# The planner of a one-core hybrid layer: its clock, its step boundaries and the start of a front

## The chip, the cores and the metric

One core of a Trainium2 chip runs the whole program in one launch. The metric is device time in microseconds (us), the median of runs of the same program, and less is better. TensorE (PE) does the matmuls, VectorE (DVE), ScalarE (ACT) and GpSimd (POOL) the rest, and SyncE (SP) issues most of the DMAs.

## The reference, cut to what matters

One layer for a prompt of 16 + 1024 rows and a sample of 64 rows, all in fp32, the model 2048 wide:

```
xn   = rmsnorm(h) * norm_w
proj = xn @ w_in                                   # 2048 -> 8208
a_b, a_c, a_x, a_z, qkv, z_b, b_logit, a_logit = split(proj)
y_a  = a_b * causal_conv3(a_c * a_x) * silu(a_z)   # mixer A, 1024 channels
q, k, v = silu(causal_conv4(qkv))                  # mixer B, 8 heads x 128
q = l2norm(q) / sqrt(128);  k = l2norm(k)
S_t = exp(g_t) (I - beta_t k_t k_t^T) S_{t-1} + beta_t k_t v_t^T ;  o_t = S_t^T q_t
y_b = rmsnorm(o) * o_norm_w * silu(z_b)
h   = h + concat(y_a, y_b) @ w_out
y   = rmsnorm(h) * final_norm_w
```

The recurrence is computed in chunks: with A unit lower triangular (built from k k^T, beta and the decays), T = inverse(A), and per chunk u = T (beta v - beta exp(g) k S), o = exp(g) q S + (q k^T * decay) u, and a new S.

## The kernel before, in words

**Stages.** The 1104 rows (with a gap, 1152) are three pieces of three 128-row chunks, and they are kept transposed (features on partitions) in a high and a low fp32r half, as are the weights: a product is three matmuls (xh*wh, xl*wh, xh*wl). A *job* is one 128-column tile of `w_in` for all three pieces: 16 k-steps of nine matmuls into three PSUM tiles `pj` (four banks in all). Weight chunks of four k-steps come as `wr` by SP, ACT makes `wh` and DVE `wl` (`Weights.split`). When a job ends, `post` evicts its `pj` tiles on DVE and starts a generator (`a_tile`, `b_tile`, `z_tile`) for the convolution and the SiLU, whose result goes to DRAM (`scr`, `yscr`). At the end three passes of `block` multiply by `w_out`, `evac` adds the residual, and `finish` makes the final norm. For the last 512 columns the `w_out` tiles are loaded and split ahead by `after(1, ...)`: `wq`, then `wa`/`wb` (k below 12) or a free corner of `yh` (k from 12).

**The delta rule** runs between the projection's matmuls, 24 times (8 heads x 3 pieces), as a front and a back. `dn_front(h, p)` loads k and q (`kq`), transposes q (`psq`) and k (`psk`) on PE, takes sums of squares on ACT (`accum_out`, tile `ss`), and works out the scales on DVE (`rsqrt_of`, `cq`, `kn`); then masks `bm` and `at`, the products `psm`, and the 32x32 inverses: `bm` goes to DRAM (`e_in`), POOL eliminates in 30 steps, and the result comes back into `t32`. `dn_back(h, p)` reads `t32`, builds the 128x128 inverse (`psx`, `psy`), runs three chunks of the state (`psr`, `psu`, `psn`, `po`), then takes the norm of `po`: sums of squares on ACT (`jk`, `so2`, which the rows call `so`), fifteen small DVE operations (the first reads `so2`, the last makes `ro`, called `roy` in the rows) and `on`; then it transposes `on` on PE (`pot`) and multiplies by `zg`. The PSUM pool `psd` has three banks, and the one of `po` is its own.

**What sets the order.** Each engine works its instructions off in order. The DVE's order is the one in which the Python code issues them. The generators are interleaved by a planner: `clk` holds a planned time of PE, DVE and ACT. `mm` and `tr` add to `clk["pe"]`; `Timed` (V and S) adds a fixed part and a part per element to DVE's or ACT's. After each k-step of nine matmuls, `pump` advances every generator whose due time has come (`running[k][0] <= clk["pe"]`); a `yield d` sets the next due time to `max(clk.values()) + d`. Convolution steps are pumped while DVE's planned time is less than 0.7 us ahead of PE's, and what is left of them at the end of a job is issued there, ahead of the next evictions (`flush_convs`). A back may start when the planned end of POOL's work is reached (`EL`, `el_done`); a front f when `f - backs[0] <= 1`, `backs[0]` being the number of backs that have ended.

Of the kernel before, what the change touches and what calls it, by code (L numbers as in the profile page):

```python
# [8 lines left out]
F32 = mybir.dt.float32  # L9
# [8 lines left out]
P = 128  # L18
# [7 lines left out]
NG = 3 * NH  # L26
# [19 lines left out]
class Timed:  # L46
# [5 lines left out]
    def __getattr__(self, name):  # L52
        fn = getattr(self._e, name)

        def call(out, *a, **k):
            n = 1
            for d in out.shape[1:]:
                n *= d
            c = self._c
            c[self._k] = max(c[self._k], c["pe"]) + self._f + n * self._p  # L60
            return fn(out, *a, **k)  # L61

        return call
# [3 lines left out]
def hymba_kernel(ctx: ExitStack, tc: tile.TileContext, hT, x_prompt, x_sample, w_in, w_ba, w_out, cst1, cst2, par,  # L67
                 s_delta, fnw, y_p, y_s, o_ca, o_cq, o_dp, o_ds):
    nc = tc.nc
    clk = {"pe": 0.0, "dve": 0.0, "act": 0.0}  # L70
    V = Timed(nc.vector, clk, "dve", 0.09, 0.00104)
    S = Timed(nc.scalar, clk, "act", 0.2, 0.00083)
    G, T, Q = nc.gpsimd, nc.tensor, nc.sync

    def mm(out, lhsT, rhs, start, stop):
        n = 1
        for d in rhs.shape[1:]:
            n *= d
        if lhsT.dtype == F32R:
            clk["pe"] += max(n / 2400 + 0.003, 0.107)  # L80
        else:
            clk["pe"] += 4 * max(n, lhsT.shape[1]) / 2400
        T.matmul(out, lhsT, rhs, start=start, stop=stop)  # L83

    def tr(out, in_, idn):
# [53 lines left out]
    def rsqrt(y, t, v):  # L139

        V.tensor_scalar(t.bitcast(I32), v.bitcast(I32), 1, None, ALU.logical_shift_right)
        V.tensor_scalar(y.bitcast(I32), t.bitcast(I32), -1, 0x5F3759DF, ALU.mult, ALU.add)
        for _ in range(3):
            V.tensor_tensor(t, y, y, ALU.mult)
            V.scalar_tensor_tensor(t, t, -0.5, v, ALU.mult, ALU.mult)
            V.scalar_tensor_tensor(y, t, 1.5, y, ALU.add, ALU.mult)

# [20 lines left out]
    gens = []  # L168
    done = set()
    fronts, backs, el_done, front_of, state = [0], [0], {}, {}, {}  # L170
    running = {}
    pool_free = [0.0]

# [9 lines left out]
    def pump():  # L183
        while True:
            moved = False
            f, b = fronts[0], backs[0]
            if "gate" in done and "front" not in running and f < NG and f - b <= 1:
                h, p = divmod(f, 3)
                if (KQ, h, p) in done and (QQ, h, p) in done:
                    running["front"] = [0.0, dn_front(h, p)]  # L190
            if "back" not in running and b < f and b < NG and el_done.get(b, 1e9) <= clk["pe"]:
                h, p = divmod(b, 3)
                if (VQ, h, p) in done and (ZQ, h, p) in done:
                    running["back"] = [0.0, dn_back(h, p)]
            for k in list(running):
                if running[k][0] <= clk["pe"]:
                    moved = True
                    if not step(running[k]):
                        del running[k]
                        if k == "back":  # L200
                            backs[0] += 1
                        elif k == "front":
                            fronts[0] += 1
            if not moved:
                break
        while convs and clk["dve"] - clk["pe"] < 0.7:
            if not step(convs[0]):
                convs.popleft()
# [245 lines left out]
    with ExitStack() as pro:  # L454
# [80 lines left out]
        a, n = PIECES[0]  # L535
# [108 lines left out]
    with ExitStack() as pro:  # L644
# [10 lines left out]
        for p in range(3):  # L655
            a, n = PIECES[p]
# [99 lines left out]
    dn = net.enter_context(tc.tile_pool(name="dn", bufs=1))  # L756
# [6 lines left out]
    def psd(name):  # L763
        return pd.tile([P, 4, P], F32, tag="pd", name=name)

    EL = (5.0, 45.0)
    t32 = [dn.tile([P, 3, P], F32, tag=f"t32_{i}", name=f"t32_{i}") for i in range(2)]
    for i in range(2):
        V.memset(t32[i], 0.0)
# [2 lines left out]
    def dn_front(h, p):  # L772

        kq = tmp("kq", "kq", 2, (P, 3, 2, P))
        for i, w in ((0, KQ), (1, QQ)):
            Q.dma_start(kq[:, :, i, :], scr[h][w][p].rearrange("p (c t) -> p c t", t=P))
        gr = tmp("gr", "gr", 1)
        r0 = h * NCH + 3 * p
        Q.dma_start(gr, gscr[None, r0:r0 + 3, :].to_broadcast([P, 3, P]))
        yield 2.1  # L780
        c3 = slice(3 * p, 3 * p + 3)
        ss = dn.tile([P, 6], F32, tag="ss", name="ss", bufs=2)
        jk = dn.tile([P, P], BF16, tag="jk", name="jk")
        pq_ = psd("psq")
        for c in range(3):
            tr(pq_[:, c, :], kq[:, c, 1, :], ident)
        for c in range(3):
            S.activation(jk, pq_[:, c, :], AF.Square, accum_out=ss[:, 3 + c:4 + c])
        yield 0.0
        pk_ = psd("psk")  # L790
        for c in range(3):
            tr(pk_[:, c, :], kq[:, c, 0, :], ident)
        for c in range(3):
            S.activation(jk, pk_[:, c, :], AF.Square, accum_out=ss[:, c:c + 1])
        V.tensor_scalar(ss, ss, 4 * EPS, None, ALU.add)
        rq = rsqrt_of(dn, ss, 6, "rq")


        cq = dn.tile([P, 12], F32, tag="cq", name="cq", bufs=2)
        V.tensor_scalar(cq[:, 0:3], rq[:, 3:6], float(P) ** -0.5, None, ALU.mult)  # L800
        V.tensor_tensor(cq[:, 3:6], hb[:, h, c3], rq[:, 0:3], ALU.mult)
        V.tensor_tensor(rq[:, 3:6], rq[:, 0:3], rq[:, 0:3], ALU.mult)
        V.tensor_tensor(cq[:, 6:9], nbeg[:, h, c3], rq[:, 3:6], ALU.mult)
        V.tensor_tensor(cq[:, 9:12], nb[:, h, c3], rq[:, 3:6], ALU.mult)
        kn = tmp("kn", "kn", 2)
        V.tensor_tensor(kn, pk_[:, 0:3, :], kds[:, h, c3, None].to_broadcast([P, 3, P]), ALU.mult)
        km = None
        if p == 0:
            km = dn.tile([P, P], F32, tag="km", name="km")
            V.tensor_scalar(km, pk_[:, 0, :], kdm[:, h:h + 1], None, ALU.mult)  # L810
        yield 0.0

        bm = tmp("bm", "bm", 2)
        for c in range(3):
            cc = 3 * p + c
            V.scalar_tensor_tensor(bm[:, c, :], gr[:, c, :], gc[:, h, cc:cc + 1], cst[:, C_MS:C_MS + P], ALU.subtract,
                                   ALU.max)
        S.activation(bm, bm, AF.Exp, scale=-1.0)
        at = tmp("at", "at", 2)
        for c in range(3):  # L820
            cc = 3 * p + c
            V.scalar_tensor_tensor(at[:, c, :], gr[:, c, :], gc[:, h, cc:cc + 1], cst[:, C_MT:C_MT + P], ALU.subtract,
                                   ALU.min)
        S.activation(at, at, AF.Exp)
        S.activation(gr, gr, AF.Exp)
        if p == 0:

            V.memset(bm[64:P, 0, 0:64], 0.0)
            V.memset(at[0:64, 0, 64:P], 0.0)
        yield 0.0  # L830
        for c in range(3):
            pm = psd("psm")
            mm(pm[:, 0:2, :], kq[:, c, 0, :], kq[:, c, :, :], True, True)
            V.scalar_tensor_tensor(bm[:, c, :], pm[:, 0, :], cq[:, 9 + c:10 + c], bm[:, c, :], ALU.mult, ALU.mult)
            V.tensor_tensor(at[:, c, :], pm[:, 1, :], at[:, c, :], ALU.mult)
            yield 0.0
        yield 1.4

        eT = dn.tile([12, 32, 32], F32, tag="eT", name="eT", bufs=1)
        i = (3 * h + p) % 2  # L840
        Q.dma_start(whole(e_in[i]), bm)
        G.dma_start(eT, blocks(e_in[i]))  # L842
        tm = dn.tile([12, 240], F32, tag="tm", name="tm", bufs=1)
        for j in range(1, 31):
            n = 31 - j
            t = tm[:, 0:n * j].rearrange("m (i r) -> m i r", r=j)
            G.tensor_tensor(t, eT[:, j + 1:32, j:j + 1].to_broadcast([12, n, j]),  # L847
                            eT[:, j:j + 1, 0:j].to_broadcast([12, n, j]), ALU.mult)
            G.tensor_tensor(eT[:, j + 1:32, 0:j], eT[:, j + 1:32, 0:j], t, ALU.add)  # L849
        G.dma_start(blocks(e_out[i]), eT)  # L850
        G.dma_start(t32[i], whole(e_out[i]))
        yield 0.3

        V.tensor_tensor(kq[:, :, 1, :], kq[:, :, 1, :], gr, ALU.mult)
        front_of[h, p] = (kq, kn, km, at, cq, bm)
        pool_free[0] = el_done[3 * h + p] = max(clk["pe"] + EL[0], pool_free[0]) + EL[1]

    def dn_back(h, p):
        kq, kn, km, at, cq, bm = front_of.pop((h, p))
# [51 lines left out]
        for c in range(3):  # L911
# [31 lines left out]
            mm(po[:, c, :], kq[:, c, 1, :], s, False, True)  # L943
            state[h] = sn
            yield 0.2
        if p == 2:
            Q.dma_start(o_dp[h], state[h])

# [1 line left out]
        jk = dn.tile([P, P], BF16, tag="jk", name="jk")  # L950
        for c in range(3):
            S.activation(jk, po[:, c, :], AF.Square, accum_out=ss[:, c:c + 1])
        V.tensor_tensor(ss, ss, cq[:, 0:3], ALU.mult)
        V.scalar_tensor_tensor(ss, ss, 1.0 / P, cq[:, 0:3], ALU.mult, ALU.mult)
        V.tensor_scalar(ss, ss, EPS, None, ALU.add)
# [301 lines left out]
```

## Time and profile before

| | |
|---|---|
| median of 3 runs (lowest, highest) | 2252.47 us (2252.29, 2257.59) |
| the profiled execution | 2251.76 us; its span is 2250.0 us, so 1.76 us lie around it |
| PE busy | 2188.0 us, 97% |
| DVE, ACT, POOL busy | 1361.8 (61%), 602.4 (27%), 875.4 us (39%) |
| mean granted TensorE clock | 0.994 of full speed |

A PE matmul's record overlaps the next one (records of 340 ns follow each other every 174 ns), so PE's busy time says that little is idle, not how fast it goes. Times within the span are counted from its start. The clock of TensorE has two levels, 2.4 GHz (1.00) and 1.2 GHz (0.50).

### The profile page before, as it was taken

The page shows a single profiled execution, that of the slowest core. Times are in us where ns is not written, and L with a number is a line of the kernel's source. Part 1 is how long each engine was busy: PE and PEld are TensorE (multiplying, and loading weights), DVE is VectorE, ACT ScalarE, POOL GpSimd, SP SyncE. Part 2 cuts the span into 40 slices and gives each one's busy share as a digit, 9 for nine tenths or more (in the row PEclk, how much of TensorE's full clock was granted, in tenths as well). Part 3 has the DMA queues.
Part 4 walks back from the last instruction along what each step waited for, and adds up shares of the span by engine and source line. Part 5 has one row for each costly group of instructions (what it writes and reads, how often), then busy time and mean ns, then how long its engine had stood idle before and what let it go on. Part 6 is the DMA issues. An engine that isn't in the chain of part 4 may idle for free. (4 is left out here: it accounts for less than half of the span.)

```text
span 2250.0 us, 35424 instructions
## 1 busy us (share of the span) xinstructions
PE 2188.0 (97%) x12794; PEld 2071.4 (92%) x12794; DVE 1361.8 (61%) x3540; ACT 602.4 (27%) x1483; POOL 875.4 (39%) x1516
## 2 busy tenths in 40 slices
PE   8999999999999999999999999999999999999997
PEld 8999899999999999999999999999999997788886
DVE  6653475777585556665775567675645345474644
ACT  7232121222222212212222222222221125444341
POOL 0000038475556566666657655657473000000000
PEclk9999999999999999999999999999999999999999
DMA  7223132222222122223232223232221228664652
GB/s 262 78 87 94 39 92 81 84 86 89 84 88 81 56 81 88 81 59 90 72 99 64 81 75 87 85 87 78 72 74 53 94 82 279 207 198 145 225 166 85
DMA packets 162067, 231.12 MB, mean 103 GB/s; under 512 B 17756, under 2 KB 89636, under 8 KB 161764
## 3 DMA queue, kind: packets, MB, share of 16 engines
q1 hardware_dynamic: 156356, 217.30, 31.2%
q0 software_dynamic: 3072, 7.11, 1.7%
q10 hardware_dynamic: 2464, 4.46, 0.5%
q8 instruction: 100, 1.64, 0.3%
q14 instruction: 75, 0.61, 0.1%
HBM read 184.61 MB, written 44.17 MB: 102 GB/s over the span
## 5 line engine op out<-in xcount | busy, mean ns | idle before, releaser
L83 PE MATMUL pj<-xh,wh 128*128 128x384 f32 x2048 | 694.9, 340 | 11.5 <-DVE raw L61 3.9
L83 PE MATMUL pj<-xl,wh 128*128 128x384 f32 x2048 | 692.4, 338 | 1.3 <-DVE xl L61 1.3
L83 PE MATMUL pj<-xh,wl 128*128 128x384 f32 x2048 | 691.3, 338 | 0.0
L61 DVE TENSOR_TENSOR wl<-wr,wh 128x512 fp32r<-128x512 f32 x464 | 335.5, 725 | 343.6 <-ACT wh L61 341.0
L83 PE MATMUL pj<-x,wh 128*128 128x320 f32 (+3 forms) x2048 | 519.2, 333 | 6.6 <-ACT x L61 6.6
L61 ACT CAST wh<-wr 128x512 fp32r<-128x512 f32 x464 | 285.8, 618 | 845.5 <-PE pj L83 626.7
L847 POOL TENSOR_TENSOR tm<-eT 12x30 f32<-12x30 f32 (+4 forms) x720 | 399.6, 555 | 121.7 <-DMA eT<-e_in 67.1
L849 POOL TENSOR_TENSOR eT<-eT,tm 12x30 f32<-12x30 f32 (+4 forms) x720 | 422.9, 587 | 56.4
L83 PEld LDWEIGHTS pj<-xh,wh 128*128 128x128 f32 x2048 | 387.2, 189 | 17.3 <-DVE xt L61 4.8
L83 PEld LDWEIGHTS pj<-xl,wh 128*128 128x128 f32 x2048 | 387.0, 189 | 2.9 <-DVE xl L61 2.2
L83 PEld LDWEIGHTS pj<-xh,wl 128*128 128x128 f32 x2048 | 386.8, 189 | 0.0
L83 PEld LDWEIGHTS pj<-x,wh 128*128 128x128 f32 x2048 | 349.3, 190 | 12.6 <-ACT x L61 6.7
L83 PE MATMUL pj<-x,wl 128*128 128x320 f32 (+3 forms) x1024 | 320.4, 313 | 5.2 <-DVE wl L61 5.2
L842 POOL DMA_DIRECT2D eT<-e_in x24 | 17.2, 716 | 578.2 <-DMA wr<-in_w_in 310.8
L83 PE MATMUL po<-wh,yh 128*128 128x512 f32 x656 | 238.9, 396 | 1.6 <-DVE yh L61 1.5
L83 PE MATMUL po<-wl,yh 128*128 128x512 f32 x528 | 208.9, 396 | 1.8 <-DVE wl L61 1.7
L83 PEld LDWEIGHTS pj<-x,wl 128*128 128x128 f32 x1024 | 193.3, 189 | 7.1 <-DVE wl L61 6.6
L83 PEld LDWEIGHTS po<-wh,yh 128*128 128x128 f32 x656 | 123.1, 188 | 32.9 <-DVE yh L61 2.7
L61 DVE SCALAR_TENSOR_TENSOR acc<-raw,pk,acc 128x384 f32<-128x384 f32 (+1 forms) x216 | 147.1, 681 | 6.0
L83 PE MATMUL po<-wh,yl 128*128 128x512 f32 x336 | 132.8, 395 | 0.0
L83 PEld LDWEIGHTS po<-wl,yh 128*128 128x128 f32 x528 | 99.1, 188 | 27.5 <-DVE wl L61 4.0
L61 ACT ACTIVATE raw<-acc 128x384 f32<-128x384 f32 (+1 forms) x72 | 36.8, 512 | 154.2 <-DVE acc L61 154.2
(242 smaller groups left out, 2127.9 us busy)
## 6 DMA issues: line engine op xcount, KB each, us to landing
wr<-in_w_in SPq DMA_DIRECT2D x288, 256.0 KB, 3.1
wr<-in_w_out SPq DMA_DIRECT2D x176, 256.0 KB, 2.8
scr<-acc SPq DMA_DIRECT2D x48, 192.0 KB, 1.9
kq<-scr SPq DMA_DIRECT2D x48, 192.0 KB, 3.0
hres<-in_x_prompt SPq DMA_DIRECT2D x32, 256.0 KB, 5.4
yr<-yscr SPq DMA_DIRECT2D x32, 192.0 KB, 3.7
scr<-co SPq DMA_DIRECT2D x24, 192.0 KB, 2.4
gr<-gscr SPq DMA_DIRECT2D x24, 192.0 KB, 3.5
```

The source lines that it names most:

```text
L61: return fn(out, *a, **k)
L83: T.matmul(out, lhsT, rhs, start=start, stop=stop)
L842: G.dma_start(eT, blocks(e_in[i]))
L847: G.tensor_tensor(t, eT[:, j + 1:32, j:j + 1].to_broadcast([12, n, j]), eT[:, j:j + 1, 0:j].to_broadcast([12, n, j]), ALU.mult)
L849: G.tensor_tensor(eT[:, j + 1:32, 0:j], eT[:, j + 1:32, 0:j], t, ALU.add)
```

## The change: what it does

It changes four kinds of things, and no instruction is added or removed: each engine issues the same ones in another order.

- The planner's costs: DVE's fixed part 0.09 to 0.19 us, 0.19 us more for an ACT operation with `accum_out`, a matmul of fp32r 0.453 ns a column (before 0.417 and 3 ns), a plain fp32 matmul as two passes; `EL` from (5, 45) to (4, 48).
- The DVE work on ACT's sums of squares becomes a step of its own, in the front (`yield 0.2`; the `yield 0.0` between `psq` and `psk` goes) and in the norm of the back (`yield 0.2` behind the squares).
- A front f may start when `f - freed[0] <= 1`; `freed[0]` counts the backs whose three state chunks have been issued, so it may run beside the norm of a back. `cq` gets a third buffer.
- The wait ahead of the front's `e_in` store: 1.4 to 0.2.

```diff
-            c[self._k] = max(c[self._k], c["pe"]) + self._f + n * self._p
+            c[self._k] = max(c[self._k], c["pe"]) + self._f + n * self._p + ("accum_out" in k) * 0.19
...
-    V = Timed(nc.vector, clk, "dve", 0.09, 0.00104)
+    V = Timed(nc.vector, clk, "dve", 0.19, 0.00104)
...
-            clk["pe"] += max(n / 2400 + 0.003, 0.107)
+            clk["pe"] += max(n * 0.000453, 0.107)
         else:
-            clk["pe"] += 4 * max(n, lhsT.shape[1]) / 2400
+            clk["pe"] += 2 * max(n * 0.00086, 0.107)
...
+    freed = [0]
...
-            if "gate" in done and "front" not in running and f < NG and f - b <= 1:
+            if "gate" in done and "front" not in running and f < NG and f - freed[0] <= 1:
...
-    EL = (5.0, 45.0)
+    EL = (4.0, 48.0)
...
             S.activation(jk, pq_[:, c, :], AF.Square, accum_out=ss[:, 3 + c:4 + c])
-        yield 0.0
         pk_ = psd("psk")
...
             S.activation(jk, pk_[:, c, :], AF.Square, accum_out=ss[:, c:c + 1])
+        yield 0.2
         V.tensor_scalar(ss, ss, 4 * EPS, None, ALU.add)
...
-        cq = dn.tile([P, 12], F32, tag="cq", name="cq", bufs=2)
+        cq = dn.tile([P, 12], F32, tag="cq", name="cq", bufs=3)
...
-        yield 1.4
+        yield 0.2
...
+        freed[0] += 1
         if p == 2:
...
             S.activation(jk, po[:, c, :], AF.Square, accum_out=ss[:, c:c + 1])
+        yield 0.2
         V.tensor_tensor(ss, ss, cq[:, 0:3], ALU.mult)
```

**DVE at the norm of a back** (head 1, piece 0; `sn` is the new state of its last chunk, `so_...` the sums of squares, `acc` a convolution, `wl` a weight half). Before:

```order
L61 TENSOR_TENSOR wl<-wr,wh 128x512
L61 SCALAR_TENSOR_TENSOR sn<-sn,egl,psn 128x128
L61 TENSOR_TENSOR so_5441<-so_5441,cq 128x3
L61 SCALAR_TENSOR_TENSOR so_5441<-so_5441,cq 128x3
L61 TENSOR_SCALAR so_5441<-so_5441 128x3
L61 TENSOR_SCALAR rot<-so_5441 128x3
```

and after the change:

```order
L61 SCALAR_TENSOR_TENSOR sn<-sn,egl,psn 128x128
L61 SCALAR_TENSOR_TENSOR acc<-raw,acc 128x384
L61 TENSOR_SCALAR acc<-raw,pk 128x384
L61 SCALAR_TENSOR_TENSOR acc<-raw,pk,acc 128x384
L61 TENSOR_TENSOR wl<-wr,wh 128x512
L61 SCALAR_TENSOR_TENSOR acc<-raw,pk,acc 128x384 x2
L61 TENSOR_TENSOR so_5539<-so_5539,cq 128x3
```

Six rows of convolution and weights now stand between the last state and the first operation that reads ACT's sums. On PE the transposes `pot` of this back move with it: 23 `pj` matmuls stood between its last `po` and its first `pot`, now 72 do. Over the 24 backs it was 23, 27 and 27 in three and 45 or 54 in the others, and is now 60 to 81.

**PE at the start of a front** (the front of head 1, piece 1). Before:

```order
L87 MATMUL psq<-cst,kq 128x128 x3
L83 MATMUL pj_5407<-x_241,wh 128x336 x2
L83 MATMUL pj_5407<-x_241,wl 128x336
L83 MATMUL pj_5408<-xh_244,wh 128x384
L83 MATMUL pj_5408<-xl_245,wh 128x384
L83 MATMUL pj_5408<-xh_244,wl 128x384
L83 MATMUL pj_5409<-xh_1310,wh 128x384
L83 MATMUL pj_5409<-xl_1311,wh 128x384
L83 MATMUL pj_5409<-xh_1310,wl 128x384
L87 MATMUL psk<-cst,kq 128x128 x3
```

and after the change:

```order
L83 MATMUL pj_5387<-xh_1310,wl 128x384
L87 MATMUL psq<-cst,kq 128x128 x3
L87 MATMUL psk<-cst,kq 128x128 x3
L83 MATMUL pj_5385<-x_241,wh 128x336 x2
L83 MATMUL pj_5385<-x_241,wl 128x336
L83 MATMUL pj_5386<-xh_244,wh 128x384
```

The nine matmuls between the two transposes went away. From the third front on, `psq` also stands nearer to the last `po` matmul of the back that frees its `kq` buffer (two fronts earlier): 63 or 72 `pj` matmuls lay between in 20 of 22 cases, now 36 do in 19.

**DVE ahead of the last pass** (`hres<-po` are the three evictions that end the pass before the last, `wb` and `yh<-wq` the splits of the last weights). Before:

```order
L61 TENSOR_TENSOR wb<-wq,wa 128x512 x2
L61 TENSOR_TENSOR hres_22007<-po_22614,hres_22007 128x512
L61 TENSOR_TENSOR hres_22007<-po_22615,hres_22007 128x512
L61 TENSOR_TENSOR hres_22007<-po_22616,hres_22007 128x512
L61 TENSOR_TENSOR hres_22007<-hres_22007,fw 128x512
L61 TENSOR_TENSOR wb<-wq,wa 128x512 x2
L61 TENSOR_TENSOR yh_21193<-wq,yh_21193 128x2x256 x4
```

and after the change:

```order
L61 TENSOR_TENSOR wb<-wq,wa 128x512
L61 TENSOR_TENSOR hres_22007<-po_22612,hres_22007 128x512
L61 TENSOR_TENSOR hres_22007<-po_22613,hres_22007 128x512
L61 TENSOR_TENSOR hres_22007<-po_22614,hres_22007 128x512
L61 TENSOR_TENSOR hres_22007<-hres_22007,fw 128x512
L61 TENSOR_TENSOR wb<-wq,wa 128x512 x3
L61 TENSOR_TENSOR yh_21254<-wq,yh_21254 128x2x256 x4
```

Seven of the sixteen weight tiles are now split behind those evictions, one more than before. `wq` has two buffers, so five loads (before: four) wait for a split that stands there.

## Rows read from the trace of the kernel before

**Rows 1.** The chain that ended last: start us, us, engine, tile, count of instructions.

```profile
1641.39 7.47 PE pj L83 x45
```

**Rows 2.** Waits of PE: waiting tile, what ended the wait, us in total, times, longest.

```profile
PE pot L87 <- DVE on L61: 8.9, 4, 2.9
...
PE pj L83 <- DVE wl L61: 5.2, 4, 2.1
PE pj L83 <- DVE raw L61: 3.9, 4, 2.0
PE pj L83 <- DVE cs L61: 3.6, 3, 1.3
PE psx L83 <- DVE b L61: 3.2, 3, 1.3
PE pj L83 <- DVE xt L61: 3.1, 5, 0.9
```

**Rows 3.** Stretches of low clock: from:to, length, busy PE, PEld, DVE, ACT, POOL, PEclk, DMA.

```profile
290.93:294.34 3.41, 3.22 (x11) 3.22 (x12) 2.75 (x6) 0.52 (x1) 0.00 (x0) 0.50 0.86 253
577.65:581.06 3.41, 3.08 (x11) 3.08 (x12) 3.19 (x8) 0.67 (x2) 3.02 (x6) 0.50 0.19 58
697.12:703.95 6.83, 6.01 (x20) 6.01 (x21) 5.34 (x12) 1.52 (x3) 5.97 (x11) 0.50 0.43 144
820.00:823.41 3.41, 3.41 (x12) 3.41 (x11) 3.41 (x8) 0.00 (x0) 3.14 (x4) 0.50 0.45 125
1372.96:1376.37 3.41, 3.41 (x13) 3.41 (x12) 3.34 (x10) 0.00 (x0) 0.00 (x0) 0.50 0.29 82
```

**Rows 4.** Timeline of one back's norm: start us, us, engine, line, instruction, wait.

```profile
571.01 0.39 PE L83 MATMUL po<-sn,kq 128*128 128x128 f32 x2
572.64 0.16 DVE L61 TENSOR_TENSOR so<-so,cq 128x3 f32<-128x3 f32 x1 [1.30 <-ACT jk L61]
577.37 0.56 DVE L61 TENSOR_TENSOR on<-po,roy 128x384 f32<-128x384 f32 x1
577.98 0.47 PE L87 MATMUL pot<-cst,on 128*128 128x128 f32 x1 [2.92 <-DVE on L61]
```

**Rows 5.** Waits of DVE, all engines' view: the front's norm chain.

```profile
DVE ss L61 <- ACT jk L61: 79.8, 22, 5.8
```

**Rows 6.** Timeline: from POOL's input to the back's first reads on DVE.

```profile
1143.48 0.39 SPq L841 DMA_DIRECT2D e_in<-bm  x1
1195.47 0.78 POOL L851 DMA_DIRECT2D t<-e_out  x1 [2.94 <-DVE cs L61]
1201.06 0.55 DVE L61 TENSOR_TENSOR t<-t,cst 128x384 f32<-128x384 f32 x1
1202.15 0.52 DVE L61 TENSOR_TENSOR b<-bm,cst 128x384 f32<-128x384 f32 x1
```

**Rows 7.** The tile t32 (named t): landing of its loads and stores.

```profile
DMA to landing us min/median/max: 2.8/3.0/4.8
```

**Rows 8.** Timeline of DVE and SP ahead of the last pass.

```profile
2206.92 1.29 DVE L61 TENSOR_TENSOR wb<-wq,wa 128x512 fp32r<-128x512 f32 x2
2207.68 6.04 SPq L1138 DMA_DIRECT2D wq<-in_w_out  x4
2216.93 0.69 DVE L61 TENSOR_TENSOR yh<-wq,yh 128x512 fp32r<-128x512 f32 x1 [0.26 <-ACT yh L61]
```

**Rows 9.** Timeline of SP: the two kq loads of one front; and page, DMA issues.

```profile
1346.53 0.52 SPq L776 DMA_DIRECT2D kq<-scr  x1
...
1350.57 0.52 SPq L776 DMA_DIRECT2D kq<-scr  x1
...
kq<-scr SPq DMA_DIRECT2D x48, 192.0 KB, 3.0
```

**Rows 10.** DVE's weight halves by form, 400 to 1700, and 1750 to 1840 us.

```profile
L61 DVE TENSOR_TENSOR wl<-wr,wh 128x512 fp32r<-128x512 f32 x177 | 136.4, 771 | 54.8 <-ACT wh L61 54.6
...
L61 DVE TENSOR_TENSOR wl<-wr,wh 128x512 fp32r<-128x512 f32 x14 | 9.7, 692 | 38.1 <-ACT wh L61 38.1
```

## The prediction, made before the changed kernel was run

> **What bounds the kernel now.** I read the page first: PE is busy for 97% of the span, and the change neither adds nor removes a matmul, so only the few per cent in which PE waits or runs slowly can move. The chain that ended last gives the pace of undisturbed work: 45 `pj` matmuls in 7.47 us, 0.166 us each [rows 1]. Next I read the waits of PE alone, because waits of other engines count only where they end in one of these. The reader should see that nearly all of them end on DVE, in three families [rows 2]: `pot` waits for the norm of a back (8.9 us, in only 4 of 24 backs), `psx` waits for `b`, the first thing that a back makes on DVE (3.2 us), and the projection waits for an eviction (`raw`, `cs`, `xt`: 10.6 us) or for a weight half `wl` (5.2 us). Third, the granted clock by stretches: five times it fell to 0.50 (1.2 GHz), each time with a longer PE wait just before or at its start [rows 3]. Last, the timeline of one long `pot` wait, to see which work is late [rows 4].
>
> A sum has to be made against the profiled execution, 2251.76 us (its span and 1.76 us around it); it lies 0.7 us below the median of the three runs. I take 0.3%, 6.8 us, as what a measurement of this kernel can tell from no change.
>
> **The norm of the back: 8.9 us and the clock behind it.** The last `po` matmuls end at 571.40. ACT's sums let DVE begin at 572.64, fifteen small operations take until `on` starts at 577.37, `on` ends at 577.93, and `pot` starts at 577.98: 6.6 us from `po` to `pot` with nothing else on DVE in between [rows 4]. PE had only 23 matmuls to put there, 3.8 us, and stood still for 2.9 us. The other two long waits are the backs with 27 matmuls in the order, and with 45 (7.5 us) one wait is left, which is small because the three long ones take all but a little of the 8.9 us [rows 2]. After the change the fewest is 60 matmuls, 10.0 us. DVE now has convolution work ahead of the chain; that may be some 3 us and still fits, so I take the whole 8.9 us as gained (bounds 6 and 8.9).
>
> Three of the slow stretches belong to these waits: 577.65, 697.12 and 820.00, 13.65 us together. At 0.166 us they would hold 82 matmuls, and they hold 43 [rows 3]: 39 x 0.166 = 6.5 us. About 1.1 us of it is standing still, counted already (the two rows where PE is busy for less than the stretch by 0.33 and 0.82 us). That leaves 5.4 us, which goes with the waits (bounds 3.5 and 5.4).
>
> **The start of the back: 2.7 us.** A back's first three DVE operations, from `t` at 1201.06 to the end of `b` at 1202.67, take 1.6 us [rows 6]. The planner counted 3 x (0.09 + 0.40) = 1.5 us for them and will count 3 x (0.19 + 0.40) = 1.8 us, so that `psx` comes at least one group of nine matmuls later where it stood too near. Of the 3.2 us [rows 2] I take 2.7 (bounds 0 and 3.2).
>
> **Evictions and weight halves: 8 of 18.4 us.** A job's second piece reuses the bank that the previous job's first piece leaves, so a DVE that is late by about a microsecond at the end of a job stops PE. DVE stands idle for 79.8 us in 22 fronts waiting for ACT's sums, up to 5.8 us at a time, with everything queued behind it [rows 5]; putting that work behind a step of its own lets convolutions and evictions pass. The norm chain of the front itself is not split, so an eviction that lands just behind it is still late. The waits are 10.6 us for evictions, and the slow stretch at 1372.96 (13 matmuls where 20.5 fit) adds 1.2; for `wl` they are 5.2 us, and the one at 290.93 (11 of 20.5, less 0.2 us of standing) adds 1.4 [rows 2, 3]. I take about half, 5.5 + 2.5 = 8 us. The bounds are 0 (the late places only move) and 18.4.
>
> **The last pass: 3 us lost.** The planner's PE time per 512 columns grows from 0.216 to 0.232 us, its DVE time too, and `after` comes out one weight tile behind: five `wq` loads instead of four wait behind the evictions of the pass before. With two buffers, loads go in pairs: the first pair is issued from 2207.68, the fourth load at 2213.72 (2207.68 + 6.04), and the last split ends at 2217.62 [rows 8]. A fifth load must wait for the third load's split, about 1 us before that end, and itself takes a landing, a cast and a split, about 4 us by the same rows (2213.72 to 2217.62 is 3.9). So the last split ends near 2220.6, 3.0 us later, and PE, which has used up the other tiles, waits for it (bounds 1.5, if the earlier ones come sooner, and 5, with a drop of the clock).
>
> **kq: 2 us lost.** A front's loads wait for the last `po` of the back two pieces earlier, then land. Now 36 matmuls (6.0 us) instead of 63 (10.4) cover this. With the loads at once after `po`, 0.6 us apart and 3.0 us to land, 3.6 to 4.2 us are needed and nothing shows. But SP works in order, and in one front a `scr` store and a `wr` load came between: the second load was issued 4.0 us after the first and would land about 7 us after `po` [rows 9]. `psq` reads just this second load. If three or four of 22 fronts are that late, 2 to 4 us; I take 2 (bounds 0, and 24 if all 22 were 1.1 us late).
>
> **POOL's trip: 3 us lost.** From `e_in` (1143.48) POOL's result leaves at 1195.47 and DVE reads it at 1201.06 [rows 6]. The landing takes 2.8 to 4.8 us [rows 7], so 0.8 to 2.8 us were to spare. This is one of the closest backs: 282 `pj` matmuls stand between the last `bm` and the first read. Three of 24 backs had fewer than 290, and after the change eight have (269 to 286); the median goes from 309 to 300, so 1.5 us of cover is gone. A late result stops DVE at `t`, behind it a weight half and convolutions, and on PE `psx`. I take three backs with 0.6 us each and one drop of the clock, 1.2 us as at 1372.96: 3 us (bounds 0, and the rival below).
>
> The rest hides. `e_in` is issued 1.2 us earlier, on SP alone. The six squares of the front now follow each other on ACT; what they delay there are weight casts that are made a chunk ahead. The bank of `psk` is held through the step, and two of three banks are enough for a back, whose product is always read before the next but one is asked for; were that cover gone, each `psm` or `psr` would wait for the front's chain.
>
> **Sum.** 8.9 + 5.4 + 2.7 + 8.0 = 25.0 gained, 3.0 + 2.0 + 3.0 = 8.0 lost: 2251.76 - 17.0 = 2234.8, so 2235 us, 17.5 us under the median.
>
> **Rivals.**
> *The late places only move.* DVE has the same work, and each of its chains stays whole; evictions and `wl` halves gain nothing and new waits eat what the starts of the backs and part of the clock give back. For it speaks that only 4 of 24 backs wait for `pot` at all and that the rest of PE's waits are scattered; against it that the `pot` term is fixed by the order. 8.9 + 5.4 gained, 8 lost with some 4 of new waits: about 2249 us, no change.
> *All DVE lateness goes.* Evictions, `wl` and `psx` waits vanish with the 79.8 us of DVE's standing, and nothing is late on `kq` and POOL: 8.9 + 5.4 + 3.2 + 18.4 - 3.0 = 32.9, about 2219 us. Against it: the unsplit chains.
> *POOL's result becomes late.* The trip from `e_in` to the first read is what the backs wait for, in place of `pot`. It decides from about 4 us of lengthening: then the eight near backs wait 3 us each, eight more 1 us, and each of the first eight brings a slow stretch of 1.2 us: 24 + 8 + 10 = 42 lost on top of the sum, about 2277 us. For it speaks the spare of 0.8 to 2.8 us; against it that the trip does not depend on the order, but for what DVE and POOL do to each other. DVE's `wl` took 771 ns while POOL worked and 692 ns when POOL was done [rows 10], so the two do slow each other on one side at least. The Trainium skill (GPSIMD Engine Reference, Key points) says why: the two share SBUF interfaces, and DVE instructions with two SBUF inputs are among those that contend. That rule speaks against the change, since it puts such instructions where DVE stood waiting beside POOL. By it, were POOL slowed as DVE is (11%) through 79.8 us spread over 24 trips, a trip would grow by 0.4 us, far from 4; no row here shows POOL's side.
>
> **Chances and range.** My forecast, 2226 to 2246: 0.58. Only moved, 2246 to 2255: 0.20. All lateness gone, 2212 to 2226: 0.13. POOL late, or `kq` late in most fronts, above 2259: 0.09. The range holds 8 in 10: from 2222 (part of the third case stays out) to 2252 (most of the second is in), and it takes in the bounds of the terms as long as they do not all fall on one side; the likeliest case alone has 2226 to 2246. Below 2245.7 is faster, above 2259.2 slower: 0.71, 0.20 and 0.09.
>
> **What would show it.** In the waits of PE, `pot<-on` should be gone, `psx<-b` below 1 us, evictions and `wl` together about half; `ss<-jk` on DVE should fall from 79.8 to below 25 us. The granted clock should have no slow stretch near a `pot`. In the last pass five `wq` loads should follow the evictions and PE's wait there be some 3 us longer. `psq` waiting for a DMA, or DVE's `t` waiting for `t<-e_out`, show the two losses, with their sizes. I am wrong if `pot` still waits (DVE has more ahead of the chain than 3 us), if `psq` waits in most fronts, if slow stretches appear at new places, or if the evictions wait as long as before.

## The result: slower by 0.6%

The changed kernel took 2266.52 us in the median (2263.45 to 2272.73), the kernel before 2252.47 us; the ratio is 1.006 (95% interval 1.0046 to 1.0074). The prediction, 2235 us, has the wrong sign, and the time lies outside its range. The changed kernel's profiled execution is its fastest one, 2263.45 us with a span of 2261.7 us, so the traces differ by 11.7 us.

Where they went is seen first in the waits of PE after the change, which answer to [rows 2] (columns: what waited, what ended the wait, us in total, times, the longest):

```profile
PE pj L83 <- DVE raw L61: 20.7, 9, 4.2
PE pj L83 <- DVE zr L61: 8.0, 4, 3.8
PE pj L83 <- DVE wl L61: 3.0, 4, 1.3
...
PE pj L83 <- DVE cs L61: 1.8, 1, 1.8
PE rsx L83 <- DVE dg L61: 1.7, 1, 1.7
PE psq L87 <- DMA kq<-scr: 1.7, 1, 1.7
PE pj L83 <- DVE za L61: 1.6, 1, 1.6
PE po L83 <- ACT yh L61: 1.0, 1, 1.0
PE pj L83 <- DVE xt L61: 0.6, 2, 0.4
```

The waits of `pot` for `on` and of `psx` for `b` have no row any more, and `wl` fell from 5.2 to 3.0 us: three families went as forecast. But the evictions (`raw`, `zr`, `cs`, `za`, `xt`) wait for 20.7 + 8.0 + 1.8 + 1.6 + 0.6 = 32.7 us where they waited for 11.5 (10.6 of [rows 2], and 0.9 for `za`). That one family took back more than all that the others gave. All PE waits of the two traces add up to 51.1 us before and 59.1 after, 8.0 us more. The rest of the 11.7 us is the clock, as the next rows show.

The granted clock fell to 0.50 nine times, not five [rows 3] (columns as there; the slow last 7 us of both kernels are left out, here and in all sums of slow stretches):

```profile
347.07:350.48 3.41, 3.41 (x13) 3.39 (x12) 2.66 (x6) 0.62 (x2) 3.10 (x5) 0.50 0.46 135
722.53:725.94 3.41, 3.41 (x13) 3.41 (x12) 1.57 (x5) 0.16 (x1) 0.78 (x1) 0.50 0.43 80
842.00:845.41 3.41, 3.41 (x13) 3.27 (x11) 1.35 (x5) 0.00 (x0) 0.78 (x1) 0.50 0.21 45
1080.93:1084.34 3.41, 3.04 (x10) 3.07 (x11) 3.38 (x17) 0.00 (x0) 1.76 (x5) 0.50 0.19 15
1115.07:1118.48 3.41, 3.41 (x12) 3.11 (x12) 2.29 (x8) 0.00 (x0) 3.10 (x5) 0.50 0.09 27
1316.45:1319.86 3.41, 3.09 (x12) 2.93 (x12) 2.89 (x13) 1.10 (x6) 2.94 (x7) 0.50 0.02 5
1350.59:1354.00 3.41, 3.41 (x13) 3.41 (x12) 2.56 (x8) 0.00 (x0) 2.94 (x7) 0.50 0.13 38
1470.05:1473.46 3.41, 2.89 (x9) 2.92 (x10) 3.36 (x15) 0.00 (x0) 2.86 (x8) 0.50 0.18 62
60.35:63.76 3.41, 3.41 (x13) 3.41 (x12) 3.34 (x13) 1.46 (x2) 0.00 (x0) 0.50 0.08 28
```

None lies at a `pot` any more. Eight stand at the end of a job, at a wait for an eviction, and the one at 60.35 in the prologue. They last 30.7 us together, where it was 20.5; as half the clock does half the work, the 10.2 us more cost about 5 us (an estimate).

At the longest of the waits, and at five others, convolution work is late. DVE's timeline at the end of that job (start us, us, engine, line, instruction, and in brackets its idle time before):

```profile
1462.92 0.41 DVE L61 TENSOR_SCALAR acc<-raw,pk 128x384 f32<-128x384 f32 x1
1463.37 1.93 DVE L61 SCALAR_TENSOR_TENSOR acc<-raw,pk,acc 128x384 f32<-128x384 f32 x3
1465.89 0.56 DVE L61 SCALAR_TENSOR_TENSOR acc<-raw,acc 128x384 f32<-128x384 f32 x1 [0.59 <-ACT raw L61]
1466.36 0.41 DVE L61 TENSOR_SCALAR acc<-raw,pk 128x384 f32<-128x384 f32 x1
1466.81 1.93 DVE L61 SCALAR_TENSOR_TENSOR acc<-raw,pk,acc 128x384 f32<-128x384 f32 x3
1469.33 0.56 DVE L61 SCALAR_TENSOR_TENSOR acc<-raw,acc 128x384 f32<-128x384 f32 x1 [0.59 <-ACT raw L61]
1469.80 0.62 DVE L61 TENSOR_TENSOR raw<-pj,rs 128x256 f32<-128x256 f32 x3
```

And PE's, at the same place:

```profile
1470.57 0.66 PE L83 MATMUL pj<-xh,wh 128*128 128x384 f32 x1 [4.20 <-DVE raw L61]
1471.02 0.52 PE L83 MATMUL pj<-xl,wh 128*128 128x384 f32 x1
1471.34 0.52 PE L83 MATMUL pj<-xh,wl 128*128 128x384 f32 x1
```

Two whole pieces of a convolution, 6.9 us of DVE (1462.92 to 1469.80), stand ahead of the evictions (the row at 1469.80) that PE waits for; and since nothing else is left to put between them, each also waits 0.59 us for its own tanh on ACT. After the wait the matmuls start 0.45 and 0.32 us apart, at 1.2 GHz, where 0.166 us is the pace of undisturbed work [rows 1]. The Python code puts convolution steps there in `flush_convs`, at a job's end. The plan's clocks can be followed without a chip: nine of the 56 jobs that run beside fronts and backs end with convolution steps that are not yet issued, of 12 pieces in all, where the plan before had none.

It is not so at every late eviction. Of the 13 eviction waits of over 1 us in this trace, six (16.5 us) have convolution steps on DVE ahead of the eviction, but seven (14.5 us) have the chain of a front or of a norm there, and four of the eight slow stretches are of this second kind (722.53, 842.00, 1080.93 and 1316.45). This is the one at 1316.45, where the wait is 2.28 us; the first two rows are the end of a norm's chain:

```profile
1314.67 0.16 DVE L61 SCALAR_TENSOR_TENSOR rot<-rot,so 128x3 f32<-128x3 f32 x1
1314.87 0.42 DVE L61 SCALAR_TENSOR_TENSOR roy<-rot,roy 128x3 f32<-128x3 f32 x1
...
1315.52 0.56 DVE L61 TENSOR_TENSOR on<-po,roy 128x384 f32<-128x384 f32 x1
1316.00 0.63 DVE L61 TENSOR_TENSOR raw<-pj,rs 128x256 f32<-128x256 f32 x3
```

Before the change the three eviction waits of over 1 us (4.6 us) all had a front's chain ahead of the eviction, and none had convolution steps.

That gave theory 1: the dearer planned cost of DVE makes the rule that issues a step while DVE's planned time is less than 0.7 us ahead issue fewer steps, and `flush_convs` puts the rest ahead of the evictions. Rivals were theory 2 (fronts beside norms put two chains of small operations one behind the other), theory 3 (any new number deals the late places out anew, with no direction) and, from the second set of runs, theory 4 (a long wait is DVE's lateness coming due, so that only less DVE work gets rid of it).

### The profile page after: what moved, and what is told of

It reads as the page before. It is cut to its first block, busy times and chain, and to the rows that moved or that the text cites. A ratio compares the mean times of both kernels' runs of the same rounds, so it can differ in the third digit from the quotient of the medians.

```text
span 2261.7 us, 35420 instructions
## 1 busy us (share of the span) xinstructions
PE 2191.7 (97%) x12794; PEld 2078.7 (92%) x12794; DVE 1374.5 (61%) x3540; ACT 602.6 (27%) x1483; POOL 877.6 (39%) x1516
## 4 chain that ended last, share of the span: by engine, by line
PE 86%; DVE 8%; issue 1%; ACT 1%; DMA 1%; SPq 0%; DVEq 0%; ACTq 0%
PE pj L83 60%; PE po L83 17%; DVE acc L61 2%; PE psx L83 1%; PE psy L83 1%; PE psm L83 1%; DVE wl L61 1%; PE psn L83 1%; PE pjb L83 1%; PE psr L83 1%; PE psu L83 1%; DVE rot L61 1%; DVE roy L61 0%; DVE rqt L61 0%; DMA yr<-yscr 0%
## 5 line engine op out<-in xcount | busy, mean ns | idle before, releaser
L83 PE MATMUL pj<-xh,wh 128*128 128x384 f32 x2048 | 696.8, 341 | 32.9 <-DVE raw L61 20.7
```

## The experiments

All times are medians, with the ratio to the kernel before on the same chip, whose median there was 2254.3 to 2255.4 us. Waits and slow stretches are those of the one execution that was traced; in runs 1, 4 and 5 it was the longest of its kernel, 3 to 5 us above the median.

**1. DVE's cost back.** The changed kernel with

```diff
-    V = Timed(nc.vector, clk, "dve", 0.19, 0.00104)
+    V = Timed(nc.vector, clk, "dve", 0.09, 0.00104)
```

> The changed kernel with DVE's planned fixed cost back at 0.09 us; all its other edits stay. Theory 1 (convolution steps held back): the dearer cost makes the planner count DVE as busy, so that it issues fewer convolution steps, and what is left at a job's end goes ahead of the job's evictions (12 steps in 9 of 56 jobs; none with 0.09). Then the evictions' waits of PE fall from 33 us to 10 to 15, the slow stretches of the clock from 9 to 5 or fewer, and the time to 2230 to 2245 us, since pot stays without a wait. Theory 2 (two chains): fronts beside norms stack the chain of a norm and that of the next front on DVE, whatever it is counted at; the evictions stay above 25 us and the time above 2258. Theory 3 (new deal): every change of the planner's numbers deals the late places out anew; waits of 10 to 35 us, no direction to be told, 2240 to 2270.

2245.82 us, 0.9966 (0.9953 to 0.998). One number is worth the whole loss and more: 1.006 to 0.9966 is 0.94%, 21 us. Theory 2, with 2258 us and more, is refuted in this form; theory 1 had at most 2245 us, and theory 3's wide range holds the time as well. The evictions wait for 13.7 us, and all four waits of over 1 us (9.3 us) stand behind the chain of a front or a norm, none behind convolution steps. Two things came otherwise than theory 1 said: `pot` waits for 2.8 us, and the traced execution has seven slow stretches in place of five or fewer (27.3 us in all, 30.7 in the changed kernel, 20.5 before). But it is the longest of the seven executions; over all of them the mean granted clock is 0.993 to 0.996 here, 0.994 in the middle, and 0.990 to 0.992 in the changed kernel, 0.991 in the middle. By this estimate some 7 of the 21 us are the clock (0.003 of 2250 us).

**2. The old rule for fronts.** The changed kernel with

```diff
-            if "gate" in done and "front" not in running and f < NG and f - freed[0] <= 1:
+            if "gate" in done and "front" not in running and f < NG and f - b <= 1:
```

> The changed kernel with the old rule for fronts: the next front starts only when the back two before it has ended, norm and all. Theory 1: the plan still leaves convolution steps at job ends (14 in 12 jobs), so evictions wait for 25 to 40 us and the time stays at 2260 to 2272 us. Theory 2: without a front beside the norm the two chains no longer meet; the evictions fall to 10 to 18 us and the time to 2240 to 2252. Theory 3: no direction.

2323.74 us, 1.0314 (1.0299 to 1.0329): 57 us worse than the changed kernel, which none of the theories foresaw. The evictions wait for 37.6 us, so theory 2 does not explain them. Most of the rest comes at the end, where the waits of DVE show a new row:

```profile
DVE t L61 <- DMA t<-e_out: 20.8, 1, 20.8
```

With the changed planned times the fronts come so late that the last back's trip through POOL outlasts the projection. PE has nothing left and waits 23.1 us for `b`, and the clock is at 0.50 for 58.03 us there. The rule for fronts beside norms is what keeps the changed kernel from this.

**3. Convolution steps earlier.** The changed kernel with

```diff
-        while convs and clk["dve"] - clk["pe"] < 0.7:
+        while convs and clk["dve"] - clk["pe"] < 2.0:
```

> The changed kernel, in which a convolution step is issued when DVE's planned clock is up to 2.0 us ahead of PE's, not 0.7 us. Theory 1: no step is left at any job's end, the evictions' waits fall from 33 to 12 to 20 us and the time to 2238 to 2252 us, although every planned cost is that of the changed kernel. Theory 2: the meeting chains stay, the evictions stay above 25 us, the time above 2258; a longer queue on DVE may even add to it. Theory 3: no direction.

2269.47 us, 1.0068 (1.0056 to 1.008): no gain. No step is left at any job's end, and the evictions did fall, to 20.1 us, near the upper end of what theory 1 said. But other work on DVE now comes late:

```profile
PE pj L83 <- DVE raw L61: 12.6, 4, 3.5
PE pj L83 <- DVE wl L61: 9.9, 5, 6.5
PE psr L83 <- DVE sn L61: 6.7, 3, 3.6
PE psu L83 <- DVE r L61: 4.7, 3, 1.8
PE pot L87 <- DVE on L61: 3.6, 1, 3.6
```

`wl` (in its longest wait), `sn` and `r` now stand behind convolution steps; the one wait for `on`, at the end of the projection, is for the norm's own chain. The time expected from theory 1 did not come: to issue the steps early costs as much as to hold them back. All PE waits add up to 64.3 us, and the slow stretches to 44.4 us (59.1 and 30.7 in the changed kernel).

**4. Only pot later.** The kernel before with

```diff
-        yield 3.2
+        yield 6.0
         pot = psd("pot")
```

> The kernel before with one edit: the step ahead of pot waits 6.0 planned us in place of 3.2. It prices the first two terms of the prediction by themselves. If they were right: no wait of pot for on is left (8.9 us before), the three slow stretches behind such waits go (5.4 us), and the time falls by 14 us to about 2238. If a wait that goes only appears elsewhere: evictions and other waits grow by as much and the time stays within 7 us of 2252.

2254.7 us, 1.0004 (0.9996 to 1.0013): nothing. `pot` waits no more, as wanted, and this is what waits instead:

```profile
PE pj L83 <- DVE raw L61: 12.3, 6, 2.9
PE pj L83 <- DVE wl L61: 6.9, 8, 2.1
PE psx L83 <- DVE b L61: 4.7, 5, 2.5
PE pj L83 <- DVE cs L61: 3.9, 2, 3.1
PE psu L83 <- DVE r L61: 3.7, 3, 1.9
```

Evictions went from 11.5 to 19.5 us (with `xt`, `za` and `ya`), `wl` from 5.2 to 6.9, `psx` from 3.2 to 4.7 and `psu` from 2.3 to 3.7: 12.6 us more for the 8.9 that went, and 23.9 us of slow clock instead of 20.5. (Some 3 us of this are those of a long execution.) The back that ends later starts the next front later. In two of the seven eviction waits of over 1 us a front's chain has got between a job's end and its eviction, in the other five a norm's chain. This is the longer of the two, 2.85 us:

```profile
660.52 0.17 DVE L61 TENSOR_SCALAR ss<-ss 128x6 f32<-128x6 f32 x1 [4.64 <-ACT jk L61]
660.73 0.17 DVE L61 TENSOR_SCALAR rqt<-ss 128x6 int32<-128x6 int32 x1
...
663.95 0.34 DVE L61 TENSOR_SCALAR km<-psk,kdm 128x128 f32<-128x128 f32 x1
664.21 0.63 DVE L61 TENSOR_TENSOR raw<-pj,rs 128x256 f32<-128x256 f32 x3
```

**5. The left-over steps behind the evictions.** The changed kernel, costs and all; `project` leaves out its `flush_convs`, and `project_all` issues the left-over steps between the evictions (the old order stays for the jobs of `hold` in the prologue and for those with a piece `AC` of mixer A):

```diff
...
+            left = len(convs)
+            for i, (key, ps) in enumerate(got.items()):
+                while left > 2 - i:
+                    if not step(convs[0]):
+                        convs.popleft()
+                        left -= 1
+                post(*key, ps)
```

> The changed kernel, in which convolution steps that are left at a job's end go behind the job's first one or two evictions (as far as three raw buffers allow) and no longer ahead of all of them. The plan has such steps in 9 of 56 jobs, 12 pieces, in both. Theory 1 (the steps that are held back cost the time, by their place ahead of the evictions): the evictions' waits fall from 33 us by 8 to 15, two to four slow stretches go with them, and the time falls from 2266 to 2245 to 2256 us. Theory 3 (new deal, whatever stands there): the DVE has the same work, the waits come at the second or third eviction or at the next weight half, and the time stays at 2260 to 2270.

2253.14 us, 0.9997 (0.9986 to 1.0007): 0.63%, 14 us better than the changed kernel, by 12 pieces of work moved past one or two evictions each. The evictions fell to 23.1 us and the slow stretches to 23.9. The wait of 4.20 us shown above has become this one:

```profile
1463.32 0.41 PE L83 MATMUL pj<-xh,wh 128*128 128x384 f32 x1 [1.42 <-DVE raw L61]
```

So theory 1 holds for 14 of the 21 us. Of the other 7 us some 4 lie in the prologue, whose flushes this run leaves as they are (that they are the cause is not shown): the gate's first `pjb` starts at 241.56 in the changed kernel and at 241.76 here, at 237.10 before and at 237.44 in run 1; that is where `rsx` waits 1.7 us for `dg` and the stretch at 60.35 stands. The rest fits what theory 1 does not cover: the seven eviction waits behind the chain of a front or a norm are still there (14.9 us, 14.5 in the changed kernel, and 9.3 in run 1). So DVE's planned cost also moved those chains; by which of the planner's rules is open.

**6. DVE's cost alone.** The kernel before with

```diff
-    V = Timed(nc.vector, clk, "dve", 0.09, 0.00104)
+    V = Timed(nc.vector, clk, "dve", 0.19, 0.00104)
...
         while ready[0] < min(i + 2, NK):
+            if i > 10:
+                flush_convs()
             step(y0)
```

> The kernel before with DVE's planned fixed cost at 0.19 us in place of 0.09 and nothing else of the change (besides a call that issues the last convolution steps ahead of the last pass's first block, without which this plan never ends). The plan leaves 25 convolution pieces in 18 jobs' ends, twice as many as the changed kernel. Theory 1: evictions wait for more than in the changed kernel, 35 to 55 us, and the time is 2270 to 2300. Theory 3: no direction; 2245 to 2275. If the cost of 21 us that the first runs gave to this number were a matter of its company (fronts beside norms, the other costs), it would be within 7 us of 2252.

2367.65 us, 1.0504 (1.0487 to 1.0522), far worse than any theory had it. The evictions wait for 45.3 us, inside theory 1's 35 to 55, and 30.7 of them in eight waits of over 1 us that have convolution steps ahead of the eviction; `pot` waits for 24.3. And the end is that of run 2, worse: DVE waits 24.9 us for `t<-e_out`. The number alone does both kinds of harm; the other edits of the change hide the second.

**7. The steps alone.** The kernel before with

```diff
-        yield 0.0
         pk_ = psd("psk")
...
             S.activation(jk, pk_[:, c, :], AF.Square, accum_out=ss[:, c:c + 1])
+        yield 0.2
...
             S.activation(jk, po[:, c, :], AF.Square, accum_out=ss[:, c:c + 1])
+        yield 0.2
```

> The kernel before with the steps of the changed one behind ACT's squares, in the front and in the norm, and nothing else. It prices the term of the prediction for evictions and weight halves by itself. If that was right: DVE's wait for ACT's sums (ss<-jk) falls from 80 us to below 25, evictions and weight halves from 18 us to about 10, and the time to 2238 to 2246. If DVE only waits elsewhere, or the late places only move: ss<-jk falls as well, the waits of PE stay at 15 to 22 us, and the time within 7 us of 2252.

2246.34 us, 0.9964 (0.9953 to 0.9976): 8 us faster. `ss<-jk` fell to 34.6 us (79.8 in [rows 5]), `psx` to 1.6 and `pot` to 5.8. Evictions (15.5 us) and `wl` (4.0) together are not less than before, so the gain is not where the prediction put it, and 19.5 us is what was expected if the late places only move; the slow clock fell from 20.5 to 17.1 us.

**8. Fewer Newton steps.** The kernel before with one Newton step in place of three in every reciprocal root, which therefore come out less exact:

```diff
-        for _ in range(3):
+        for _ in range(1):
```

> The kernel before with one Newton step in place of three in each reciprocal root: a front and a norm each lose six small DVE operations, about 2 us of a chain, and the rest is computed as before. Theory 4 (a long wait of PE for a chain is DVE's lateness coming due, and a wait that is taken away at one place comes due at the next): shorter chains pay everywhere, pot's wait and the evictions' fall together, by 10 to 20 us, and the time to 2225 to 2240. Theory 3 (new deal): DVE's work is not what counts; the plan deals its places out anew, and the time stays at 2245 to 2265.

2229.73 us, 0.9894 (0.9875 to 0.9914): 24 us. Evictions wait for 8.1 us, `pot` for 1.3, and two slow stretches are left. DVE's work does count, as theory 4 says.

**9. Steps and rule for fronts, no costs.** The kernel of run 7 with, besides,

```diff
-            if "gate" in done and "front" not in running and f < NG and f - b <= 1:
+            if "gate" in done and "front" not in running and f < NG and f - freed[0] <= 1:
...
-        cq = dn.tile([P, 12], F32, tag="cq", name="cq", bufs=2)
+        cq = dn.tile([P, 12], F32, tag="cq", name="cq", bufs=3)
```

> The kernel before with the changed one's steps behind ACT's squares and its rule for fronts (with the third cq buffer), and none of its planned costs. Of this pair the steps alone were worth 8 to 9 us, and so were all the edits without DVE's cost. Theory 1 (what is gained is the steps', what is lost is DVE's cost's; the rest is worth nothing): 2241 to 2250 us, as both of these. Theory 2 in its weaker form (fronts beside norms cost something, and the other planned costs give it back): 2252 to 2262. If the rule for fronts gains by itself: below 2240.

2256.17 us, 1.0007 (0.9999 to 1.0016). Beside the steps alone, the rule for fronts costs 0.43%, some 10 us (theory 2 in its weaker form), with `wl` waiting for 11.4 us. As run 1 is this kernel plus the other planned numbers (ACT's, PE's, `EL`, the shorter `yield`), these give about 9 back.

**10. Steps and two Newton steps.** The kernel of run 7 with two Newton steps in place of three, so that the roots are less exact:

```diff
-        for _ in range(3):
+        for _ in range(2):
```

> The kernel before with the steps behind ACT's squares, and two Newton steps in place of three in each reciprocal root; the rest is computed as before. Theory 4 (PE waits for DVE's lateness, and a shorter chain pays wherever it comes due): the steps' 8 to 9 us and half of the 25 us that two Newton steps less gave, together some 20 us, 2230 to 2240 us. Theory 3 (new deal): what one edit gave need not add to the other; 2240 to 2255.

2232.51 us, 0.9904 (0.9888 to 0.9919): 22 us, where steps and half of run 8 would add up to 20. Faster than both kernels, at the price of a less exact root.

**11, 12. One Newton step in one chain only.** The kernel before, in which only the norm's call (11) or only the front's (12) asks for one step; the roots of that chain are less exact.

```diff
-        ro = rsqrt_of(dn, ss, 3, "ro")
+        ro = rsqrt_of(dn, ss, 3, "ro", 1)
...
-        rq = rsqrt_of(dn, ss, 6, "rq")
+        rq = rsqrt_of(dn, ss, 6, "rq", 1)
```

> The kernel before with one Newton step in place of three in the norm of the back alone; the rest is computed as before. The same four long waits of pot as in the run that put pot later, but here the chain behind them is about 2 us shorter and nothing is put elsewhere. Theory 4 (a wait is DVE's lateness coming due): pot's 8.9 us fall below 3, the slow stretches behind them go, nothing comes due later, and the time falls by 10 to 15 us, to 2240 to 2245. If the wait for pot is simply worth nothing: within 7 us of the kernel before.

> The kernel before with one Newton step in place of three in the front alone. No PE instruction waits for the end of this chain as pot does for the norm's; it is only in the way of evictions and weight halves. Theory 4: they fall by a third to a half, and the time by 8 to 14 us, the rest of the 25 us that both chains gave together. If only the norm's chain counts: within 7 us of the kernel before.

The norm's: 2236.06 us, 0.992 (0.9895 to 0.9944), 18 us, more than the 10 to 15 of theory 4. The front's: 2241.77 us, 0.9941 (0.9921 to 0.9962), 13 us. Run 11 against run 4 is the clearest pair of all: both take `pot`'s wait away, to 1.6 us and to nothing, but the shorter chain gains 18 us and the later `pot` none. Most of the difference is the clock: run 11 has 3.4 us of slow stretches where it was 20.5, worth some 8.5 us as above, while all its PE waits fell by only 4.1 us, from 51.1 to 47.0 (`psq` and `psx` wait for more); run 4 has more of both. In run 12 the waits that the front's chain stands in the way of fell (evictions to 6.6, `wl` to 3.9), and those for `on` stayed, as they should:

```profile
PE pot L87 <- DVE on L61: 8.2, 3, 2.9
```

## Why the prediction was wrong

The ladder of the runs, each against the kernel before: steps 0.9964; with the rule for fronts 1.0007; with all numbers but DVE's 0.9966; with DVE's 1.006. In us of 2255: -8, +10, -9, +21. Without DVE's number the change gains 8 us where the prediction had 17, so what it took as gained was too much as well.

*Evictions and weight halves: "8 of 18.4 us", bounds 0 and 18.4.* This is the step that failed. It priced what the split step lets pass and took it that the late places could at worst stay. The same edit list held a number that decides how many convolution steps are issued at all. The changed planned cost appears in the prediction only for three operations at the start of a back and for the last pass; 3540 DVE operations at 0.1 us more are 354 us more of planned DVE time in a plan whose pump stops at 0.7 us. What the pump does not issue, `flush_convs` does, ahead of an eviction. The evictions' wait grew by 21.2 us, 16.5 us of it new waits behind convolution steps, and the lower bound should have been negative. The sign follows from this one number: without it the change is 0.9966; moving the left-over steps behind evictions gave 14 us back (run 5).

*The norm: "I take the whole 8.9 us as gained", and "That leaves 5.4 us, which goes with the waits".* The wait went, as the order said. That it was a gain is refuted by run 4 for this edit on its own: a wait that is taken away by a later reader came due in other places, and slow clock with it. Run 11 shows what it is worth when DVE has less to do: 18 us, most of it the clock, which the prediction was right to price.

*The start of the back: 2.7 us.* The wait went (3.2 to no row). Its worth by itself was not measured.

*The split.* The size of the gain, 8 us, came out in run 7 by luck: the waits that shrank there are those of `psx`, `pot` and smaller ones, not of evictions and halves. `ss<-jk` did fall below 25 in the changed kernel, to 17.2 us; in run 7 it stayed at 34.6.

*The last pass: 3 us lost.* The split did come late: from the evictions that end the pass before to the end of the last split it takes 17.9 us (2214.46 to 2232.31), 14.3 before (2203.31 to 2217.62). The wait did not: PE's wait for `yh` there is 1.0 us after and 1.1 before. PE had not "used up the other tiles"; it did other matmuls of the pass meanwhile. No loss.

*kq: 2 us, POOL: 3 us.* `psq` waits once, 1.7 us, in the very first front, where no back is ahead of it: near the size by luck, by another cause. DVE never waits for `t<-e_out` in the changed kernel. The rival about POOL became true only where DVE's cost is 0.19 us and the new rule for fronts is missing (runs 2 and 6), and at the end, not in the near backs.

*The chances.* The text said that it would be wrong "if slow stretches appear at new places, or if the evictions wait as long as before". Both came. The rival "the late places only move" had the mechanism nearest to run 4, but held that new waits could eat only some 4 us.

Open: how DVE's planned cost moves the chains that stand ahead of evictions; why the clock falls so often in run 3, whose pump may run further ahead; and what in the rule for fronts costs run 9 its 10 us.

## What to carry to other kernels

In a planner a cost is also a control. Before correcting one, follow every rule that compares it with a threshold, and look at what the program does with the work that the rule then leaves over; the truer number (0.19 us is nearer to the 0.17 to 0.21 us of a small DVE operation than 0.09) can give the worse order. A wait is worth its time only if what is late gets shorter; if only its reader is put later, look for the next reader behind the same engine.

## What was not expected of the hardware

A dependent DVE operation on six columns takes 0.17 us, and the next starts 0.21 us after it (run 4, the rows at 660.52 and 660.73), where POOL does nothing (busy for 0.00 us from 660.5 to 664.0). Beside POOL's work such operations take longer: of the two rows at 1314.67 one takes 0.16 and one 0.42 us, with POOL busy for 2.91 of the 3.30 us from 1312.2. In the kernel before, the Newton steps' operations take 0.16 to 0.17 us wherever no POOL instruction overlaps them, and 0.24 us in the mean, up to 0.55, where one does. Two Newton steps less (run 8) are 360 DVE operations of 3540; DVE's busy time fell by 65 us, from 1361.8 to 1296.5, and 24 of them showed in the time. The low clock can also last far longer than the 3.41 and 6.83 us of the stretches before and after the change. In run 6, where PE had little to do at the end, one stretch holds 64.85 us with PE busy for 20.34 of them:

```profile
1878.37:1943.22 64.85, 20.34 (x73) 16.73 (x74) 15.95 (x48) 3.58 (x16) 24.49 (x46) 0.50 0.09 22
```
